# A hybrid convolution/mLSTM block on one core: x normalised in place, the width-31 convolution accumulated in PSUM, modulation sums delayed

## The chip, the cores and the metric

The kernel runs as one program on one core of a Trainium2 chip. A core has a matrix engine (PE, whose weight loads are listed as PEld), a vector engine (DVE), a scalar engine (ACT), a general engine (POOL) and a queue engine that only issues transfers (SP). Each takes its own instructions strictly in order; semaphores tie them together. The metric is the device time of one execution, in microseconds. Of the kernel before three executions were timed: median 1197.08, from 1196.81 to 1198.6. The profiled execution is a run of its own, with a time of its own.

## The reference

One layer of a diffusion block on 1024 latent tokens (1024 channels) with a prefix of 256 context tokens. Cut to what the change touches:

```
hx = modulate(rms_norm(x, norm_g[0]), mx[0], mx[1])      # mx = split(silu(c) @ w_ada + b_ada, 6)
hc = modulate(rms_norm(ctx, norm_g[0]), mc[0], mc[1])    # mc = split(silu(c_ctx) @ w_ada + b_ada, 6)
kc, vc, gtc = project_state_inputs(hc, w_in, b_gates)    # context: k, v and gates alone
a, gl, q, k, v, o, g = split(hx @ w_in + ...)            # latent tokens
u = a * sigmoid(gl)                                      # GLU, 512 channels
u = silu(layer_norm(dwconv31_along_rows_of_64(u) + conv_b))
m = bidirectional mLSTM(q, k, v, g, state from ctx)      # 4 heads, chunks of 64
x = x + mx[2] * rms_norm(concat(u, m * sigmoid(o)) @ w_out)
x = x + mx[5] * rms_norm(conv_ffn(modulate(rms_norm(x), mx[3], mx[4])))
```

Everything is float32. A matmul is run as three passes over split operands: hi x hi, hi x lo and lo x hi, with hi the value rounded to the fast matmul type and lo the rest.

## The kernel before

**Start.** The eight tiles of x (128 tokens x 1024) are loaded in two groups. For each tile ACT sums the squares (`x_sq`, L193), POOL makes the reciprocal root, DVE scales the identity by it into a 128x128 diagonal (`x_rs`, L198), and PE multiplies the tile by that diagonal (`x_tr`, L204), which transposes and normalises at once; being an ordinary float32 matmul it takes two instructions for each of 64 blocks. ACT and DVE copy the result out of PSUM (`x_evac`, L212 and L214). In between come the column sums that give the modulation of x: `mod_sum` (L228), a multiply and sum over a 128x1024 tile of `w_ada`, two for each of eight row blocks; then `mod_apply` makes hi and lo of the normalised x.

**Projection.** `glu0`, then three more GLU blocks, keep PE busy to about 127 us. A second set of 16 `mod_sum`s gives the modulation of the context. `glu_evac` (L274) leaves `u[j]`, 128 channels by 1024 tokens, for each of four channel groups j.

**Convolution.** `conv(j)` starts the accumulator `accf[:, j]` in SBUF with the centre tap and bias on ACT (L278), and adds 30 taps on DVE (L286), each a multiply and add over 16 rows of 64-|o| columns, o from -15 to 15. The four convolutions are given the lowest priority and fill DVE wherever the scheduler finds it idle; `conv_norm` reads them, at about 293 us.

**vpass(1).** PE projects v and gates, ten token tiles: eight of the latent tokens first (t = 2 to 9), then the two context tiles (t = 0, 1), 24 matmuls each (L556 and L557 with hi, L558 with lo). The context operand `hcT` is made late: DVE reads the transposed context out of PSUM and modulates it (L358, tile `h_1287` and three like it), ACT rounds it to hi (L362, tile `s_1280`), DVE subtracts to get lo (L363, tile `s_1281`). Then come vpass(0), the projection of k, the gates, the four heads, the output projection (to about 463 us), and the feed-forward part.

**Sums behind the projection.** 32 further `mod_sum`s (for mx[2] to mx[5]) are spread by `ada_step(2)`, two in each projection step of heads and output gate, and finished before the row at L325 (about 463 us).

**Order.** All engines are ordered by hand up to `glu0(0, 0, (1,))`; from there only SP is, and a list scheduler sets the order of the rest when the program is built, by priorities and its own costs. What each engine is given is fixed then, and none overtakes on the chip. PSUM has eight banks of 128x512: four of pool `mm`, four of pool `tp`.

Of the kernel before, what the change touches and what calls it, by code (L numbers as in the profile page):

```python
# [24 lines left out]
CW = 31  # L25
# [5 lines left out]
def hybrid_block(ctx: ExitStack, tc: tile.TileContext, x, cx, cc, small, gb, w_ada,  # L31
# [10 lines left out]
    wp = wide.enter_context(tc.tile_pool(name="wp", bufs=11, side="right"))  # L42
    rawp = wide.enter_context(tc.tile_pool(name="rawp", bufs=3, side="right"))
    mm = wide.enter_context(tc.tile_pool(name="mm", bufs=4, space=bass.MemoryType.PSUM))
    tp = wide.enter_context(tc.tile_pool(name="tp", bufs=4, space=bass.MemoryType.PSUM))
    early = ExitStack()
    t4 = early.enter_context(tc.tile_pool(name="t4", bufs=10))

# [33 lines left out]
    def MM():  # L82
        return mm.tile([P, 512], F32, tag="mm", name="mm")

    def TP():
        return tp.tile([P, 512], F32, tag="tp", name="tp")

    def H2(n=512):
        return sm.tile([P, 512], F32, tag="h2", name="h2", bufs=8)[:, 0:n]
# [69 lines left out]
    def load_raw(i):  # L159
        r = RAW()  # L160
        sp.dma_start(r, wblk[i])
        return r
# [21 lines left out]
    def x_load(hf):  # L184
        for t in range(4 * hf, 4 * hf + 4):
            xt[t] = T4()
            sp.dma_start(xt[t], x[t * P:(t + 1) * P, :])

    dgx = {}

    def x_sq(t):
        junk = hT[1][1][:, 2 * (t % 4):2 * (t % 4) + 2, :]
        act.activation(out=junk, in_=xt[t].rearrange("p (k n) -> p k n", k=2), func=AF.Square, accum_out=ss[:, t:t + 1])  # L193

    def x_rs(t):
        rsqrt_pow(rst[:, t:t + 1], ss[:, t:t + 1], 1, f"x{t % 2}", 1.0 / D)
        dgx[t] = H2(P)
        dve.tensor_scalar(out=dgx[t], in0=ident, scalar1=rst[:, t:t + 1], scalar2=None, op0=ALU.mult)  # L198

    def x_tr(t, ps, qs=range(4)):  # L200

        for q in qs:
            for kk in range(2):
                pe.matmul(ps[q][:, kk * 256 + t % 2 * P:kk * 256 + (t % 2 + 1) * P],  # L204
                          xt[t][:, (2 * q + kk) * P:(2 * q + kk + 1) * P], dgx[t], start=True, stop=True)

    def x_evac(pr, ps, qs=range(4)):
        for q in qs:
            dst = xT[:, 2 * q:2 * q + 2, pr * 256:(pr + 1) * 256]
            src = ps[q].rearrange("p (k n) -> p k n", k=2)  # L210
            if q % 2:
                dve.tensor_copy(out=dst, in_=src)  # L212
            else:
                act.copy(out=dst, in_=src)  # L214


    def silu_mm(dst):
        pss = MM(), MM()
        for hf in range(2):
            pe.matmul(pss[hf], ones[0:1, :], dst[0:1, hf * 512:(hf + 1) * 512], start=True, stop=True)  # L220
        return pss

    def silu_act(dst, pss):
        for hf in range(2):
            act.activation(out=dst[:, hf * 512:(hf + 1) * 512], in_=pss[hf], func=AF.Silu)
# [49 lines left out]

    def conv(j):
        uv = u[j].rearrange("p (r c) -> p r c", c=W)
        act.activation(out=accf[:, j], in_=u[j], func=AF.Identity, scale=conv_w[:, j, 15:16],  # L278
                       bias=conv_b[:, j:j + 1])
        for t in range(CW):  # L280
            o = t - 15
            if o == 0:
                continue
            lo, hi = max(0, -o), min(W, W - o)
            dst = accf[:, j].rearrange("p (r c) -> p r c", c=W)[:, :, lo:hi]
            dve.scalar_tensor_tensor(out=dst, in0=uv[:, :, lo + o:hi + o], scalar=conv_w[:, j, t:t + 1],  # L286
                                     in1=dst, op0=ALU.mult, op1=ALU.add)


    AB2 = const.tile([P, 2, 8], F32, name="AB2")  # L290
# [106 lines left out]
    with tc.manual_schedule(engines={ET.SP, ET.Activation, ET.DVE, ET.Pool, ET.PE}):  # L397
        sx = SM(1024, "G", bufs=1)
        rows[0] = sx
        sp.dma_start(sx[0:1, :], cc[0:1, :])  # L400
        x_load(0)
        mod_load(0)
        raws = load_raw(0), load_raw(1)
        x_load(1)
        pss = silu_mm(sx)
        x_sq(0)
        x_rs(0)
        pA = [TP() for _ in range(4)]
        x_tr(0, pA)
        x_sq(1)  # L410
        x_rs(1)
        x_tr(1, pA)
        silu_act(sx, pss)
        x_sq(2)
        x_rs(2)
        pB = [MM() for _ in range(4)]
        x_tr(2, pB)
        x_evac(0, pA)
        x_sq(3)
        x_rs(3)  # L420
        x_tr(3, pB)
        mod_k(0)
        x_evac(1, pB)
        x_sq(4)
        x_rs(4)
        pA = [TP() for _ in range(4)]
        x_tr(4, pA)
        mod_apply(0, 0)
        x_sq(5)
        x_rs(5)  # L430
        w = [split_blk(raws[0], dve)]
        w.append(split_blk(raws[1], dve))
        wg[0] = w
        x_tr(5, pA)
        mod_load(1)
        raws = load_raw(2), load_raw(3)
        for k in range(2, KT):
            mod_load(k)
        x_sq(6)
        x_rs(6)  # L440
        mod_sum(ada_raw[1, 1], sx, 0, 1, 1)
        x_evac(2, pA)
        x_sq(7)
        x_rs(7)
        mod_sum(ada_raw[1, 0], sx, 0, 0, 1)
# [4 lines left out]
        for q in range(4):  # L450
            x_tr(6, pA, (q,))
            x_tr(7, pA, (q,))
        mod_s(1)
        mod_apply(1, 0)
        x_evac(3, pA)
        mod_apply(0, 1)
        glu0(0, 1, (0,))
        glu0(0, 0, (1,))
    with tc.manual_schedule(engines={ET.SP}):
        mod_apply(1, 1)  # L460
        glu0(0, 1, (1,))
        wg[1] = split_blk(raws[0], pool), split_blk(raws[1], dve)
# [17 lines left out]
    accf = wide_tile(4, 2)  # L480
    vw = None
    with prio(100000):
        conv(0)
# [195 lines left out]
    def proj(i, evac):  # L679
        w = ahead.pop(i)  # L680
        n = order.index(i) + 1
        if n < len(order):
            ahead[order[n]] = load_blk(order[n])
        ada_step(2)
        for hf in range(2):
            hi, lo = hT[hf]
            ps = MM()
            yield from mm_block(ps, w, hi, lo)
            evac(hf, ps)
        return w  # L690
# [53 lines left out]
    def mlstm_head(h):  # L744
# [38 lines left out]
        for g in range(2):  # L783
# [9 lines left out]
            for t in range(4):  # L793
# [1 line left out]
                    yield from tails()  # L795
                c = 4 * g + t
                cs = slice(c * P, (c + 1) * P)
                pv, pc = TP(), TP()
                nv = pv[:, 0:258].rearrange("p (d n) -> p d n", d=2)
                nc_ = pc[:, 0:258].rearrange("p (d n) -> p d n", d=2)  # L800
                pl.matmul(pc[:, 0:258], qT[:, cs], Cs[c // 4][:, c % 4].rearrange("p d n -> p (d n)"),
# [63 lines left out]
    uf = accf  # L865

    def conv_norm():
        for hf in range(2):
            xh = [T4().rearrange("p (t n) -> p t n", n=512) for _ in range(2)]
            mv = SM(8, "cmv").rearrange("p (t s) -> p t s", s=2)  # L870
# [661 lines left out]
```

## Time and profile before

| | |
|---|---|
| median of the timed runs | 1197.08 us (1196.81 to 1198.6) |
| the profiled execution | 1197.89 us |
| its span, first to last instruction | 1195.8 us |
| PE busy | 1143.2 us, 96% |
| DVE busy | 932.0 us, 78% |
| ACT busy | 523.7 us, 44% |
| POOL busy | 121.3 us, 10% |

The profiled execution's time holds 2.1 us beside its span. A share of busy time is an average over stages with different limits: to see what a change in one stage is worth, one reads that stage's stretch of the span, which engine is full there, and which wait ends last.

### The profile page before, as it was taken

Reading aid. Unit: us, or ns where it says so; the run is one execution under the profiler, and the core shown is the slowest. Engines: PE = TensorE matmul, PEld = TensorE weight load, DVE = VectorE, ACT = ScalarE, POOL = GpSimd, SP = SyncE. Lnnn points to the kernel's source line nnn. Section 1 sums busy time; section 2 is a strip of 40 time slices with the busy share of each in tenths; the row PEclk is TensorE's granted clock in tenths of the full one; section 3 lists DMA queues with packets and bytes.
Section 4 is the critical chain, followed back from the end, with each engine's and each line's share of the span. In section 5 each row is a group of like instructions: output and inputs, shape, how many; then the busy total and the mean of one; then the engine's idle time right before and its main releaser. Section 6 shows DMA issues by size and latency. Waiting matters only on the chain.

```text
span 1195.8 us, 14940 instructions
## 1 busy us (share of the span) xinstructions
PE 1143.2 (96%) x5463; PEld 939.5 (79%) x5463; DVE 932.0 (78%) x1702; ACT 523.7 (44%) x952; POOL 121.3 (10%) x106
## 2 busy tenths in 40 slices
PE   6899898999898999999999999999999999999997
PEld 5788787877687777887787888878888878888885
DVE  4899999999779996568966676676668685995585
ACT  6432222242485454357545344343434355454461
POOL 2634120111302210010000000000000000000000
PEclk9899899999999999999999999999999999999999
DMA  8963110442225412442324231323132159633251
GB/s 305 329 207 121 52 37 1 142 147 65 88 89 176 140 56 89 150 167 89 104 73 132 88 122 55 132 89 132 45 132 93 75 192 391 227 112 117 80 220 71
DMA packets 51823, 153.42 MB, mean 128 GB/s; under 512 B 5589, under 2 KB 5925, under 8 KB 49958
## 3 DMA queue, kind: packets, MB, share of 16 engines
q1 hardware_dynamic: 40662, 132.28, 32.0%
q10 hardware_dynamic: 11088, 20.19, 4.5%
q8 instruction: 43, 0.70, 0.2%
q14 instruction: 30, 0.25, 0.1%
HBM read 123.83 MB, written 28.61 MB: 127 GB/s over the span
## 4 chain that ended last, share of the span: by engine, by line
PE 61%; DVE 6%; ACT 1%; issue 1%; POOL 0%; DVEq 0%; POOLq 0%; ACTq 0%
PE mm L1141 8%; PE mm L1143 8%; PE mm L1142 8%; PE c L1369 3%; PE c L1371 3%; PE c L1370 3%; PE tp L1143 3%; PE tp L1142 3%; PE tp L1141 3%; PE a L1369 3%; PE a L1371 3%; PE a L1370 2%; PE mm L951 2%; PE mm L953 2%; PE mm L952 2%; PE tp L508 2%
## 5 line engine op out<-in xcount | busy, mean ns | idle before, releaser
L286 DVE SCALAR_TENSOR_TENSOR s<-t,sml,s 128x864 f32<-128x864 f32 (+14 forms) x120 | 150.5, 1295 | 0.1
L150 PE MATMUL mm<-s,w 128*128 128x512 f32 (+1 forms) x320 | 126.6, 399 | 0.0
L151 PE MATMUL mm<-s,w 128*128 128x512 f32 (+1 forms) x320 | 124.7, 393 | 0.1
L133 ACT ACTIVATE w<-raw 128x1024 fp32r<-128x1024 f32 x94 | 97.0, 1054 | 20.6 <-DMA raw<-in_w_out_dram 5.3
L1141 PE MATMUL mm<-s,w 128*128 128x512 f32 x264 | 104.9, 397 | 0.7 <-ACT h L1214 0.7
L1142 PE MATMUL mm<-s,w 128*128 128x512 f32 x264 | 104.2, 395 | 0.0
L1143 PE MATMUL mm<-s,w 128*128 128x512 f32 x264 | 104.0, 395 | 0.0
L134 DVE TENSOR_TENSOR w<-raw,w 128x1024 fp32r<-128x1024 f32 x77 | 92.3, 1222 | 1.5 <-PE mm L952 0.8
L154 PE MATMUL mm<-s,w 128*128 128x512 f32 (+1 forms) x320 | 93.2, 400 | 0.0
L141 POOL TENSOR_TENSOR r<-yw,mhalf 128x1 f32<-128x1 f32 x16 | 9.7, 608 | 690.7 <-DVE yw L140 690.7
L1141 PE MATMUL mm<-x,w 128*128 128x512 f32 x176 | 70.5, 401 | 0.7 <-ACT h L1205 0.5
L151 PEld LDWEIGHTS mm<-s,w 128*128 128x128 f32 x320 | 60.9, 190 | 11.6 <-POOL s L265 0.7
L1141 PE MATMUL tp<-s,w 128*128 128x512 f32 x176 | 69.5, 395 | 0.0
L150 PEld LDWEIGHTS mm<-s,w 128*128 128x128 f32 x320 | 61.0, 190 | 10.9
L1142 PE MATMUL tp<-s,w 128*128 128x512 f32 x176 | 69.5, 395 | 0.0
L1143 PE MATMUL tp<-s,w 128*128 128x512 f32 x176 | 69.4, 394 | 0.0
L1142 PE MATMUL mm<-x,w 128*128 128x512 f32 x176 | 69.3, 394 | 0.0
L1143 PE MATMUL mm<-x,w 128*128 128x512 f32 x176 | 69.3, 394 | 0.0
L1197 DVE TENSOR_TENSOR h<-mm,h 128x512 f32<-128x512 f32 x22 | 15.2, 692 | 66.3 <-PE mm L1143 66.3
L1271 ACT ACTIVATE s<-x 128x512 fp32r<-128x512 f32 x62 | 38.4, 628 | 64.1 <-PE a L1371 25.0
L1256 DVE TENSOR_TENSOR s<-x,s 128x512 fp32r<-128x512 f32 x62 | 42.8, 695 | 29.0 <-ACT s L1271 29.0
L154 PEld LDWEIGHTS mm<-s,w 128*128 128x128 f32 x320 | 57.0, 189 | 10.2
(311 smaller groups left out, 2916.6 us busy)
## 6 DMA issues: line engine op xcount, KB each, us to landing
raw<-in_w_up_dram SPq DMA_DIRECT2D x44, 512.0 KB, 4.5
zv<-s ACTq DMA_DIRECT2D x77, 256.0 KB, 3.4
raw<-in_w_ada_dram SPq DMA_DIRECT2D x32, 512.0 KB, 4.2
t<-in_w_ada_dram SPq DMA_DIRECT2D x28, 512.0 KB, 5.8
x<-zv SPq DMA_DIRECT2D x14, 1024.0 KB, 5.0
raw<-in_wblk_dram SPq DMA_DIRECT2D x20, 512.0 KB, 4.8
d<-in_w_down_dram SPq DMA_DIRECT2D x28, 256.0 KB, 6.8
x<-zv SPq DMA_DIRECT2D x7, 768.0 KB, 4.2
```

The costliest lines, as they stand in the source:

```text
L133: act.activation(out=hi, in_=raw, func=AF.Copy)
L134: (eng or pool).tensor_tensor(out=lo, in0=raw, in1=hi.bitcast(F32), op=ALU.subtract)
L150: pe.matmul(o, w[0][:, k], hi[:, k], start=(k == 0), stop=False)
L151: pe.matmul(o, w[0][:, k], lo[:, k], start=False, stop=False)
L154: pe.matmul(o, w[1][:, k], hi[:, k], start=False, stop=(k == KT - 1))
L286: dve.scalar_tensor_tensor(out=dst, in0=uv[:, :, lo + o:hi + o], scalar=conv_w[:, j, t:t + 1], in1=dst, op0=ALU.mult, op1=ALU.add)
L1141: pe.matmul(ps, w[0][:, s], b[0][:, k], start=(start and k == 0), stop=False, skip_group_check=True)
L1142: pe.matmul(ps, w[0][:, s], b[1][:, k], start=False, stop=False, skip_group_check=True)
L1143: pe.matmul(ps, w[1][:, s], b[0][:, k], start=False, stop=(k == 3), skip_group_check=True)
L1369: pe.matmul(ps, o[:, 0, s], o[:, 2], start=start, stop=False, skip_group_check=True)
L1370: pe.matmul(ps, o[:, 0, s], o[:, 3], start=False, stop=False, skip_group_check=True)
L1371: pe.matmul(ps, o[:, 1, s], o[:, 2], start=False, stop=stop, skip_group_check=True)
```

## The change

1. PSUM. `tp` falls from four banks to two; a new pool `cv` holds one pair of banks. While no convolution runs, `TP()` hands out halves of the pair for two requests of every four. While one runs (`conv_live`), the pair is the convolution's, and head 0 takes one of its banks from `mm` (`HP()`).
2. Start of x. DVE scales the whole tile in place (128x1024), PE transposes it with the plain identity as a transpose, one instruction a block; the order of steps and of evacuations is changed; the SiLU is taken on the one row before it is spread to 128 partitions. The loads are reordered: SP issues the modulation weights ahead of the fourth weight block.
3. Convolution. The centre tap is a DVE operation from SBUF to PSUM, 29 taps read and write PSUM, the last tap (o = 1) writes `accf` in SBUF, and a 128x16 copy fills the column that it misses. There is one pair of banks, so the four convolutions follow one another.
4. Sums. `ada_step(2)` in each of twelve steps becomes `ada_step(4)` in the last six or so (`n > 5`) and none before.

```diff
-    tp = wide.enter_context(tc.tile_pool(name="tp", bufs=4, space=bass.MemoryType.PSUM))
+    tp = wide.enter_context(tc.tile_pool(name="tp", bufs=2, space=bass.MemoryType.PSUM))
+    cv = wide.enter_context(tc.tile_pool(name="cv", bufs=1, space=bass.MemoryType.PSUM))
...
+    def CV():
+        return cv.tile([P, 2, 512], F32, tag="cv", name="cv")
...
     def TP():
+        if not conv_live:
+            tp_turn[0] += 1
+            if tp_turn[0] % 4 in (3, 0):
+                if not halves_left:
+                    pair = CV()
+                    halves_left.extend((pair[:, 1], pair[:, 0]))
+                return halves_left.pop()
         return tp.tile([P, 512], F32, tag="tp", name="tp")
+    def HP():
+        return MM() if conv_live else TP()
...
-        dgx[t] = H2(P)
-        dve.tensor_scalar(out=dgx[t], in0=ident, scalar1=rst[:, t:t + 1], scalar2=None, op0=ALU.mult)
+        dve.tensor_scalar(out=xt[t], in0=xt[t], scalar1=rst[:, t:t + 1], scalar2=None, op0=ALU.mult)
...
-                pe.matmul(ps[q][:, kk * 256 + t % 2 * P:kk * 256 + (t % 2 + 1) * P],
-                          xt[t][:, (2 * q + kk) * P:(2 * q + kk + 1) * P], dgx[t], start=True, stop=True)
+                pe.transpose(ps[q][:, kk * 256 + t % 2 * P:kk * 256 + (t % 2 + 1) * P],
+                             xt[t][:, (2 * q + kk) * P:(2 * q + kk + 1) * P], ident)
...
     def silu_mm(dst):
+        act.activation(out=dst[0:1, :], in_=dst[0:1, :], func=AF.Silu)
...
     def conv(j):
         uv = u[j].rearrange("p (r c) -> p r c", c=W)
-        act.activation(out=accf[:, j], in_=u[j], func=AF.Identity, scale=conv_w[:, j, 15:16],
-                       bias=conv_b[:, j:j + 1])
-        for t in range(CW):
+        pair = CV().rearrange("p h n -> p (h n)")
+        pv = pair.rearrange("p (r c) -> p r c", c=W)
+        fv = accf[:, j].rearrange("p (r c) -> p r c", c=W)
+        dve.tensor_scalar(out=pair, in0=u[j], scalar1=conv_w[:, j, 15:16], scalar2=conv_b[:, j:j + 1], op0=ALU.mult,
+                          op1=ALU.add)
+
+        for t in (*range(15), *range(17, CW), 16):
             o = t - 15
-            if o == 0:
-                continue
             lo, hi = max(0, -o), min(W, W - o)
-            dst = accf[:, j].rearrange("p (r c) -> p r c", c=W)[:, :, lo:hi]
+            dst = (fv if o == 1 else pv)[:, :, lo:hi]
             dve.scalar_tensor_tensor(out=dst, in0=uv[:, :, lo + o:hi + o], scalar=conv_w[:, j, t:t + 1],
-                                     in1=dst, op0=ALU.mult, op1=ALU.add)
+                                     in1=pv[:, :, lo:hi], op0=ALU.mult, op1=ALU.add)
+        dve.tensor_copy(out=fv[:, :, W - 1:W], in_=pv[:, :, W - 1:W])
...
-        ada_step(2)
+        ada_step(4 if n > 5 else 0)
...
-                pv, pc = TP(), TP()
+                pv, pc = TP(), HP()
```

Lines after the change stand some 13 to 21 further down (L363 is L384, L286 is L306, L556 is L569).

**DVE, at the context operand of vpass(1), before** (`t_725` and `t_732` are the inputs of convolutions 0 and 1, which alternate):

```order
L565 COPY h_1111<-mm 128x2x2x4
L286 SCALAR_TENSOR_TENSOR s_739<-t_725,sml,s_739 128x16x57
L286 SCALAR_TENSOR_TENSOR s_739<-t_732,sml,s_739 128x16x59
L286 SCALAR_TENSOR_TENSOR s_739<-t_725,sml,s_739 128x16x56
L565 COPY h_1111<-mm 128x2x2x4
L358 TENSOR_SCALAR h_1287<-tp,AB 128x256 x2
L358 TENSOR_SCALAR h_1297<-tp,AB 128x256 x2
L363 TENSOR_TENSOR s_1281<-h_1287,s_1280 128x512
L358 TENSOR_SCALAR h_1307<-tp,AB 128x256
L363 TENSOR_TENSOR s_1281<-h_1297,s_1280 128x512
```

**DVE, the same operand after**, in two places (`t_724` is the input of convolution 1, `t_811` that of convolution 2):

```order
L578 COPY h_1111<-mm 128x2x2x4
L379 TENSOR_SCALAR h_1287<-tp,AB 128x256 x2
L379 TENSOR_SCALAR h_1297<-tp,AB 128x256 x2
L379 TENSOR_SCALAR h_1307<-tp,AB 128x256 x2
L379 TENSOR_SCALAR h_1317<-tp,AB 128x256 x2
L636 MEMSET h_1664 1x256
L306 SCALAR_TENSOR_TENSOR cv<-t_724,sml,cv 128x16x61
```

```order
L306 SCALAR_TENSOR_TENSOR cv<-t_811,sml,cv 128x16x50
L306 SCALAR_TENSOR_TENSOR cv<-t_811,sml,cv 128x16x49
L306 SCALAR_TENSOR_TENSOR s_732<-t_811,sml,cv 128x16x63
L384 TENSOR_TENSOR s_1281<-h_1287,s_1280 128x512
L384 TENSOR_TENSOR s_1281<-h_1297,s_1280 128x512
L384 TENSOR_TENSOR s_1281<-h_1307,s_1280 128x512
L384 TENSOR_TENSOR s_1281<-h_1317,s_1280 128x512
L308 COPY s_732<-cv 128x16
```

The subtractions for `s_1281` stood two places behind the modulation, with 43 taps ahead of them on DVE; they now stand behind all 90 taps of convolutions 0, 1 and 2.

**PE, at the first context tile of vpass(1), after:**

```order
L571 MATMUL mm<-w,s_118 128x272
L569 MATMUL mm<-w,s_1280 128x272 [waits Activation_49]
L570 MATMUL mm<-w,s_1280 128x272
L569 MATMUL mm<-w,s_1280 128x272 [waits DVE_49]
L570 MATMUL mm<-w,s_1280 128x272
L569 MATMUL mm<-w,s_111 128x256 [waits DVE_49]
L571 MATMUL mm<-w,s_1281 128x272 [waits DVE_49]
```

Only one matmul of a later stage (with `s_111`) has been put ahead of the one that reads `s_1281`; everything else stays behind it, as before.

**SP, the loads of the start, before** (`w` and `t_288` on are the modulation weights, `raw` the weight blocks, `t_145` to `t_151` tiles of x):

```order
L187 DMA t_151<-in_x_dram 128x1024
L243 DMA w<-in_w_ada_dram 128x1024 x2
L161 DMA raw<-in_wblk_dram 128x1024 x2
L243 DMA t_288<-in_w_ada_dram 128x1024
L243 DMA t_290<-in_w_ada_dram 128x1024
```

and after:

```order
L207 DMA t_154<-in_x_dram 128x1024
L261 DMA w<-in_w_ada_dram 128x1024 x2
L181 DMA raw<-in_wblk_dram 128x1024
L261 DMA t_162<-in_w_ada_dram 128x1024
L261 DMA t_164<-in_w_ada_dram 128x1024
L181 DMA raw<-in_wblk_dram 128x1024
L261 DMA t_168<-in_w_ada_dram 128x1024
```

The fourth weight block, which reuses the buffer of the first, has moved behind two of the modulation loads.

## Rows read from the trace of the kernel before

**Rows 1.** The page: span, then busy us, share and instructions of each engine.

```profile
span 1195.8 us, 14940 instructions
...
PE 1143.2 (96%) x5463; PEld 939.5 (79%) x5463; DVE 932.0 (78%) x1702; ACT 523.7 (44%) x952; POOL 121.3 (10%) x106
```

**Rows 2.** Busy us (instructions) of PE, PEld, DVE, ACT, POOL by stretch; clock, DMA.

```profile
120.00:164.70 44.70, 38.76 (x253) 35.81 (x251) 44.10 (x52) 11.77 (x26) 4.36 (x3) 0.92 0.12 36
164.70:220.00 55.30, 47.65 (x324) 43.95 (x324) 55.02 (x80) 13.10 (x38) 8.53 (x6) 0.94 0.06 20
220.00:308.50 88.50, 81.03 (x443) 67.64 (x441) 87.66 (x175) 26.57 (x67) 17.93 (x6) 1.00 0.36 120
308.50:463.00 154.50, 147.17 (x816) 121.73 (x817) 131.26 (x488) 89.71 (x214) 26.51 (x20) 1.00 0.36 119
```

**Rows 3.** DVE, then PE, at the context operand: start, us, instruction, idle before, releaser.

```profile
162.35 0.68 DVE L363 TENSOR_TENSOR s<-h,s 128x512 fp32r<-128x512 f32 x1
...
163.09 0.39 PE L558 MATMUL mm<-w,s 128*128 128x272 f32 x1
...
164.21 0.39 PE L556 MATMUL mm<-w,s 128*128 128x272 f32 x1 [0.35 <-ACT s L362]
...
165.05 0.39 PE L558 MATMUL mm<-w,s 128*128 128x272 f32 x1 [0.32 <-DVE s L363]
```

**Rows 4.** Convolution taps alone (L286), by stretch: DVE busy us (instructions), clock, DMA.

```profile
97.60:120.00 22.40, 21.30 (x14) 1.00 0.39 108
120.00:164.70 44.70, 34.28 (x30) 0.92 0.12 36
164.70:220.00 55.30, 45.79 (x40) 0.94 0.06 20
220.00:308.50 88.50, 49.16 (x38) 1.00 0.36 120
```

**Rows 5.** SP's longest wait up to 60 us: what waits, total, times, longest.

```profile
SPq L161 <- DVE w L134: 10.0, 1, 10.0
```

**Rows 6.** DVE by shape, whole span: form, count, busy us, mean ns, idle before.

```profile
L286 DVE SCALAR_TENSOR_TENSOR s<-t,sml,s 128x896 f32<-128x896 f32 x8 | 9.1, 1142 | 0.0
L1037 DVE TENSOR_SCALAR t<-t,r 128x1024 f32<-128x1024 f32 x8 | 6.0, 753 | 5.7 <-POOL r L141 5.7
L358 DVE TENSOR_SCALAR h<-tp,AB 128x256 f32<-128x256 f32 x8 | 3.9, 534 | 0.0
L565 DVE COPY h<-mm 128x16 f32<-128x16 f32 x10 | 1.8, 175 | 0.0
L228 DVE SCALAR_TENSOR_TENSOR raw<-raw,G 128x1024 f32<-128x1024 f32 x32 | 38.7, 1213 | 0.1
```

**Rows 7.** The same view: two operations with a PSUM source, one between SBUF tiles.

```profile
L821 DVE SCALAR_TENSOR_TENSOR h<-tp,dn,h 128x128 f32<-128x128 f32 x96 | 31.9, 345 | 0.1
L1197 DVE TENSOR_TENSOR h<-mm,h 128x512 f32<-128x512 f32 x22 | 15.2, 692 | 66.3 <-PE mm L1143 66.3
L1119 DVE TENSOR_TENSOR w<-h,w 128x512 fp32r<-128x512 f32 x22 | 15.1, 686 | 0.1
```

**Rows 8.** DVE and POOL in time, where the first taps run.

```profile
97.62 8.97 DVE L286 SCALAR_TENSOR_TENSOR s<-t,sml,s 128x784 f32<-128x784 f32 x3
...
97.60 5.51 POOL L134 TENSOR_TENSOR w<-raw,w 128x1024 fp32r<-128x1024 f32 x2 [16.47 <-ACT w L133]
```

**Rows 9.** The page's group of all 120 taps: busy us, mean ns, idle before.

```profile
L286 DVE SCALAR_TENSOR_TENSOR s<-t,sml,s 128x864 f32<-128x864 f32 (+14 forms) x120 | 150.5, 1295 | 0.1
```

**Rows 10.** PE in time, behind a wait early in vpass(1).

```profile
141.47 0.60 PE L556 MATMUL mm<-w,s 128*128 128x272 f32 x1 [3.57 <-DVE t L274]
...
142.09 0.43 PE L558 MATMUL mm<-w,s 128*128 128x272 f32 x1
```

**Rows 11.** PE's waits from 164.7 to 308.5: total us, times, longest.

```profile
PE tp L508 <- DVE h L821: 4.5, 4, 1.5
PE tp L508 <- DVE gsc L617: 3.4, 1, 3.4
```

More of the change, by code (lines that the diff above doesn't have):

```diff
@@ L83, in MM @@
         return mm.tile([P, 512], F32, tag="mm", name="mm")
-    def TP():
+    def CV():
+        return cv.tile([P, 2, 512], F32, tag="cv", name="cv")
+    conv_live = []
+    halves_left = []
+    tp_turn = [0]
+    def TP():
+        if not conv_live:
[5 more added lines that the diff above has]
+                return halves_left.pop()
         return tp.tile([P, 512], F32, tag="tp", name="tp")
+    def HP():
+        return MM() if conv_live else TP()
     def H2(n=512):
@@ L203, in x_tr, with x_evac @@
             for kk in range(2):
-                pe.matmul(ps[q][:, kk * 256 + t % 2 * P:kk * 256 + (t % 2 + 1) * P],
-                          xt[t][:, (2 * q + kk) * P:(2 * q + kk + 1) * P], dgx[t], start=True, stop=True)
-    def x_evac(pr, ps, qs=range(4)):
-        for q in qs:
+                pe.transpose(ps[q][:, kk * 256 + t % 2 * P:kk * 256 + (t % 2 + 1) * P],
+                             xt[t][:, (2 * q + kk) * P:(2 * q + kk + 1) * P], ident)
+    def x_evac(pr, ps, dq=(1, 3)):
+        for q in range(4):
             dst = xT[:, 2 * q:2 * q + 2, pr * 256:(pr + 1) * 256]
             src = ps[q].rearrange("p (k n) -> p k n", k=2)
-            if q % 2:
+            if q in dq:
                 dve.tensor_copy(out=dst, in_=src)
@@ L221, in silu_mm, with silu_rows @@
         return pss
-    def silu_act(dst, pss):
+    def silu_rows(dst, pss):
         for hf in range(2):
-            act.activation(out=dst[:, hf * 512:(hf + 1) * 512], in_=pss[hf], func=AF.Silu)
+            act.copy(out=dst[:, hf * 512:(hf + 1) * 512], in_=pss[hf])
     def mod_sum(r, s, w, ch, k):
@@ L402, in hybrid_block, with x_in @@
         mod_load(0)
-        raws = load_raw(0), load_raw(1)
+        raws = [load_raw(0), load_raw(1)]
         x_load(1)
+        mod_load(1)
+        raws.append(load_raw(2))
+        mod_load(2)
+        raws.append(load_raw(3))
+        for k in range(3, KT):
+            mod_load(k)
         pss = silu_mm(sx)
-        x_sq(0)
-        x_rs(0)
+        def x_in(t, ps):
+            x_sq(t)
+            x_rs(t)
+            x_tr(t, ps)
         pA = [TP() for _ in range(4)]
[L409 to L415, printed above, removed]
-        pB = [MM() for _ in range(4)]
[L417 to L422, printed above, removed]
+        x_in(0, pA)
+        x_in(1, pA)
+        silu_rows(sx, pss)
+        pB = [MM() for _ in range(4)]
+        x_in(2, pB)
+        x_in(3, pB)
+        x_evac(0, pA, ())
+        mod_sum(ada_raw[0, 1], sx, 0, 1, 0)
         x_evac(1, pB)
[L424 to L427, printed above, removed]
+        mod_sum(ada_raw[0, 0], sx, 0, 0, 0)
+        mod_s(0)
+        w = [split_blk(raws[0], dve)]
         mod_apply(0, 0)
-        x_sq(5)
-        x_rs(5)
-        w = [split_blk(raws[0], dve)]
         w.append(split_blk(raws[1], dve))
         wg[0] = w
[L434 to L445, printed above, removed]
         for hf in range(2):
@@ L449, in hybrid_block @@
         pA = [TP() for _ in range(4)]
[L450 to L453, printed above, removed]
+        x_in(4, pA)
+        x_in(5, pA)
+        x_evac(2, pA)
+        pA = [TP() for _ in range(4)]
+        x_in(6, pA)
+        x_in(7, pA)
+        mod_k(1)
+        x_evac(3, pA)
         mod_apply(1, 0)
-        x_evac(3, pA)
         mod_apply(0, 1)
@@ L461, in hybrid_block @@
         glu0(0, 1, (1,))
-        wg[1] = split_blk(raws[0], pool), split_blk(raws[1], dve)
+        wg[1] = split_blk(raws[2], pool), split_blk(raws[3], dve)
         for hf in range(2):
@@ L480, in hybrid_block @@
     accf = wide_tile(4, 2)
+    conv_live.append(True)
     vw = None
@@ L867, in conv_norm @@
     def conv_norm():
+        conv_live.clear()
         for hf in range(2):
```

1 line of the change is left out of this document (removed).

## The prediction

> **What bounds the kernel now.** I read the page's first part first: PE is busy 1143.2 of 1195.8 us, DVE 932.0 [rows 1]. So PE sets the time, and a change is worth what it adds to or takes from PE's idle time. The table of busy time by stretch then tells where PE is not full [rows 2]. Behind 463 us it nearly is; between 164.7 and 308.5 it is idle for 55.30 - 47.65 + 88.50 - 81.03 = 15.1 us, and there DVE is busy 55.02 + 87.66 = 142.7 of 143.8 us. The list of PE's waits there names DVE's results first [rows 11]. So from the start of the convolution to 308 us DVE is the engine that is full, and the place of one DVE instruction in its queue matters. The taps alone take DVE 150.5 us [rows 9], 94.95 of them in that stretch [rows 4].
>
> The third view is PE in time at 163 us, where vpass(1) reaches the context tiles. The first lo subtraction runs on DVE at 162.35, PE reads its result at 163.09, and PE waits 0.35 and 0.32 us for ACT and DVE in this place [rows 3]. Before, this is just in time: it has no slack to speak of.
>
> **Convolution and its place in the order: the term that decides.** The order of DVE shows the four subtractions that PE needs behind 90 taps, where they stood behind 43. PE takes its queue in order and has one matmul of a later stage ahead of the first that waits, so everything from the context tiles on waits for these taps. Nothing covers that. The start of the first subtraction, from 162.35 [rows 3]:
>
> - 47 more taps at 1.142 us, the mean of the middle size, 128x896, which is also the mean size of the 30 taps [rows 6]: +53.7.
> - Three first operations of a convolution, SBUF to PSUM, which ACT did before: no row has this form; the 128x1024 scaling between SBUF tiles takes 0.753 [rows 6]: +2.3 (with a tap's 1.142 instead, +3.4).
> - Four more context modulations at 0.534 and three more copies at 0.175 now stand ahead [rows 6]: +2.7.
> - The first 14 taps took 21.30 us, 1.52 each, the next 30 took 34.28, 1.14 each [rows 4]; while POOL worked, three took 8.97 [rows 8]. Taps with an operand in PSUM ran 345 ns a piece in 96 cases [rows 7], which leaves no room for such a stretch. I take it as gone: -5.3 (0 at the other end).
> - The start stage, below: -5.
>
> The sum is 210.8. The subtraction takes 0.7, so PE goes on at 211.5 where it went on at 163.09: +48.4. The 1.0 us or so that it loses there now is then inside the wait; I take **+47**.
>
> No row has a tap in PSUM, so 1.142 is bounded. Below: a 128x128 operation with one PSUM operand takes 345 ns and a 128x512 one 692 [rows 7], 0.904 ns an element; carried on to 896 elements this is 1.039, over 90 taps 9.3 us less. Above: the mean of all 120 taps with their stretches, 1.295 [rows 9], 13.8 us more. I keep 1.142 because PSUM as a source costs nothing at equal size: 692 against 686 ns [rows 7]. With the start at 0 or -9 us, the first subtraction comes at 197 to 230.
>
> [...]
>
> [...]
>
> **What comes back.** When PE goes on, 90 taps are done instead of 43. DVE has 30 taps, some 34 us, left where it had 94.95 [rows 4], and six sums fewer to run before `conv_norm` (8 instead of 14), 6 x 1.21 = 7.3 us [rows 6]. Its load up to `conv_norm` falls from 142.7 to about 75 us, and it no longer bounds the stretch. PE can recover its idle 15.1 us and the lower clock at 164.7 to 220, 0.94 or 6.6 us at half speed, 3.3 us [rows 2]: 18.4. The chain of the gates keeps a part of its waits (3.4 us on `gsc` alone [rows 11]), against which stand gaps too short to be listed as idle. I take **-18**, from -10 to -22.
>
> **Delayed sums.** Of the 32 sums, 20 instead of 18 now fall between `conv_norm` and the row at L325, four at the end. DVE is busy 131.26 of 154.50 us in that stretch, PE idle 7.3 [rows 2]; two sums are 2.4 us of DVE work [rows 6], part of it on the path: **+1**, from -4 to +5. The same bounds hold what two `tp` banks less cost the heads, since no row shows a bank as what a matmul waits for.
>
> **The start.** The in-place scaling costs DVE eight operations of 0.75 instead of the small ones, PE saves half of its 128 instructions, ACT a table load. SP waited 10.0 us in one piece for a buffer, with the modulation loads behind it [rows 5]; these now go ahead. So the sums that lead up to the convolution can start earlier, by at most those 10 us; DVE is their limit more than the loads, and I take 5, from 0 to 9. This is already in the sum: it does not shorten the time by itself, as PE waits at 154 or so in any case.
>
> **Sum.** 47 + 3.6 - 18 + 1 = +33.6. The profiled execution took 1197.89 us, 2.1 more than its span and 0.8 more than the median of 1197.08. 1197.08 + 33.6 gives 1230.7; I say **1231**. Ends: first subtraction at 197 and full recovery, 33 + 3.6 - 22 - 4 = +11, 1208; at 230 and little recovery, 66 + 3.6 - 10 + 5 = +65, 1262. Both ends at once are unlikely.
>
> **Rivals.**
>
> *A, faster: the taps run fast.* If operations on PSUM ran like the 128x1024 scaling, 0.753 us or 0.66 for 896 elements [rows 6], the 90 taps would end by 163. It decides from here: 210.8 less 90 x (1.142 - t) must fall to 163, t = 0.61 us. [...] Against it: a tap has two tensor sources, and such an operation with one in PSUM takes 692 ns for only 512 elements [rows 7]. Chance 0.07. [...]
>
> *B, no change that can be measured.* The wait comes, but what comes back pays for it. That needs 51 us of slack behind it; 18.4 in the stretch and PE's idle 7.3 us up to 463 [rows 2] make 25.7. So it needs taps near 0.9 us besides. Chance 0.03, at 1197 to 1200.
>
> *C, slower still.* Taps that depend on one another through a single pair of banks cannot alternate, as two convolutions do now. If each pays 0.15 us for that, the wait is 13.8 us longer (the upper end above), and if two `tp` banks also hold up the heads, little comes back: 1197 + 61 + 3.6 - 8 + 2 = 1256. For it: today only pairs alternate, and no row shows a chain alone. Against: 345 ns for 128 elements leaves no extra cost in PSUM [rows 7]. Chance 0.14.
>
> *D, the change does not do what it says:* the order of the queues is fixed, so this could only be a part of the gain at the start that does not come; it is inside the range.
>
> **How the numbers follow.** The forecast has 0.76 (1213 to 1248), A 0.07, B 0.03, C 0.14. The range of 8 in 10 leaves out A, B, most of the forecast's lowest corner and the upper part of C: 1207 to 1257. A difference of 0.2% (2.4 us) is about what a measurement of this kernel can tell from no change. Faster by more than that: A and a corner of a shorter wait, 0.09. Within it: 0.03. Slower: 0.88.
>
> **What would show it.** In the profile after, PE should have one long idle piece that starts between 150 and 160 us and ends when the line of the lo subtraction (L384) releases it, near 211. The mean of the tap group should be near 1.14 us, with no 3 us ones among the first. DVE should show free time between 212 and `conv_norm`, PE nearly none. Behind 500 us nothing should differ. If PE has no idle piece over 10 us there, the central step is wrong; if the piece is there and the time is still under 1205, what comes back was read too small; if taps are above 1.25 us, C holds.

## The result, and the profile after

The changed kernel takes 1291.28 us (1285.18 to 1293.06) against 1197.05, a ratio of 1.0775 with the interval 1.0736 to 1.0814. The direction was as forecast; the loss is 94 us, not 34, and the time lies above the range (1207 to 1257).

All views of the changed kernel are of an execution of 1285.18 us, the fastest of the four. Its page, as in [rows 1] and [rows 9], with PE's group at the wait:

```profile
span 1283.4 us, 14751 instructions
...
PE 1151.7 (90%) x5399; PEld 937.2 (73%) x5399; DVE 949.9 (74%) x1708; ACT 522.1 (41%) x950; POOL 117.5 (9%) x106
...
L306 DVE SCALAR_TENSOR_TENSOR cv<-t,sml,cv 128x784 f32<-128x784 f32 (+14 forms) x116 | 133.3, 1149 | 3.2
...
L571 PE MATMUL mm<-w,s 128*128 128x272 f32 (+1 forms) x160 | 46.9, 294 | 51.8 <-DVE s L384 51.8
```

PE has nearly the same work, and 131.7 us of its span (1283.4 - 1151.7) are idle where 52.6 were before. The table by stretch, as [rows 2], tells where (PE, PEld, DVE, ACT, POOL, then clock, DMA share, GB/s):

```profile
120.00:164.70 44.70, 36.27 (x228) 33.36 (x227) 42.81 (x52) 7.19 (x19) 3.48 (x4) 0.92 0.12 36
164.70:220.00 55.30, 5.91 (x45) 5.47 (x44) 53.03 (x49) 2.95 (x8) 0.00 (x0) 0.57 0.00 0
220.00:308.50 88.50, 85.05 (x546) 76.80 (x547) 56.26 (x97) 30.94 (x84) 14.63 (x9) 0.96 0.13 43
308.50:400.00 91.50, 83.47 (x451) 66.98 (x450) 55.72 (x183) 39.42 (x87) 17.66 (x14) 0.98 0.36 121
400.00:550.00 150.00, 122.67 (x603) 97.59 (x602) 123.19 (x422) 63.22 (x151) 15.74 (x9) 0.93 0.33 106
```

There are two holes, not one. The first is the forecast wait: PE stands from 171.7 to 223.45 us. Here are DVE and then PE in time at its end, as [rows 3]:

```profile
220.45 1.04 DVE L306 SCALAR_TENSOR_TENSOR cv<-t,sml,cv 128x784 f32<-128x784 f32 x1
221.53 1.26 DVE L306 SCALAR_TENSOR_TENSOR s<-t,sml,cv 128x1008 f32<-128x1008 f32 x1
222.71 2.49 DVE L384 TENSOR_TENSOR s<-h,s 128x512 fp32r<-128x512 f32 x4
...
223.45 0.59 PE L571 MATMUL mm<-w,s 128*128 128x272 f32 x1 [51.79 <-DVE s L384]
223.84 0.43 PE L569 MATMUL mm<-w,s 128*128 128x272 f32 x1
```

The last tap of convolution 2 (the one that writes SBUF) is followed by the four subtractions, and PE goes on. The second hole, 27 us of PE between 400 and 550, was not forecast. PE's waits there, in total, times, longest:

```profile
PE cv L521 <- DVE h L834: 15.5, 6, 8.1
PE tp L521 <- DVE h L834: 7.2, 4, 3.0
```

L521 issues the matmuls of the heads, and L834 is the instruction with which DVE reads a chunk's banks of PSUM; its output is the tile `h`. The longest case is the first scores of a group of chunks:

```profile
478.23 2.05 PE L521 MATMUL cv<-t,t 128*128 128x128 f32 x8 [8.12 <-DVE h L834]
```

Their inputs (tiles `t`) are no product of L834. What PE waits for is the *bank*. (Of the 22.7 us in the two rows, 5.6 stand before matmuls that read a tile of `h`; for these the profile alone cannot tell bank from data.)

The start of the same matmul in both traces, in microseconds, shows how the delay grows:

```
                                     before    after   later by
first matmul of vpass(1)              126.9    133.1      6.2
last matmul of vpass                  208.5    259.9     51.4
last matmul of the projections        431.5    506.6     75.1
first matmul of the gate row          462.8    541.2     78.4
first matmul of the feed-forward      537.7    622.7     85.0
last of that loop                     976.1   1063.3     87.2
```

So 51 us are there when vpass ends. Where the projections end they have become 75, at the start of the feed-forward 85: instead of 18 us coming back, 34 more are lost.

### The profile page after: what moved, and what is told of

Same layout as the page of the kernel before. It is cut to its first block, busy times and chain, and to the rows that moved or that the text cites. A ratio compares the mean times of both kernels' runs of the same rounds, so it can differ in the third digit from the quotient of the medians.

```text
span 1283.4 us, 14751 instructions
## 1 busy us (share of the span) xinstructions
PE 1151.7 (90%) x5399; PEld 937.2 (73%) x5399; DVE 949.9 (74%) x1708; ACT 522.1 (41%) x950; POOL 117.5 (9%) x106
## 4 chain that ended last, share of the span: by engine, by line
PE 57%; DVE 10%; DMA 3%; ACT 3%; issue 1%; POOL 1%; DVEq 0%; POOLq 0%; ACTq 0%
PE mm L1155 7%; PE mm L1157 7%; PE mm L1156 7%; DMA raw<-in_w_ada_dram 3%; PE c L1385 3%; PE c L1384 3%; PE c L1383 3%; PE a L1385 2%; PE a L1384 2%; PE a L1383 2%; PE mm L965 2%; PE mm L966 2%; PE mm L967 2%; PE cv L521 1%; PE tp L1155 1%; PE tp L1156 1%
## 5 line engine op out<-in xcount | busy, mean ns | idle before, releaser
L170 PE MATMUL mm<-s,w 128*128 128x512 f32 (+1 forms) x320 | 131.5, 414 | 7.4 <-ACT s L282 4.3
L306 DVE SCALAR_TENSOR_TENSOR cv<-t,sml,cv 128x784 f32<-128x784 f32 (+14 forms) x116 | 133.3, 1149 | 3.2
L171 PE MATMUL mm<-s,w 128*128 128x512 f32 (+1 forms) x320 | 128.0, 403 | 0.9 <-POOL s L283 0.9
L571 PE MATMUL mm<-w,s 128*128 128x272 f32 (+1 forms) x160 | 46.9, 294 | 51.8 <-DVE s L384 51.8
L174 PE MATMUL mm<-s,w 128*128 128x512 f32 (+1 forms) x320 | 89.7, 397 | 0.0
L170 PEld LDWEIGHTS mm<-s,w 128*128 128x128 f32 x320 | 62.7, 196 | 19.4 <-ACT s L282 4.9
L171 PEld LDWEIGHTS mm<-s,w 128*128 128x128 f32 x320 | 62.6, 196 | 13.0 <-POOL s L283 2.3
L571 PEld LDWEIGHTS mm<-w,s 128*128 128x128 f32 x160 | 31.4, 197 | 52.0 <-DVE s L384 52.0
L174 PEld LDWEIGHTS mm<-s,w 128*128 128x128 f32 x320 | 57.5, 190 | 11.1
L154 POOL TENSOR_TENSOR w<-raw,w 128x1024 fp32r<-128x1024 f32 x17 | 44.8, 2643 | 162.1 <-ACT w L153 40.0
```

The source lines that it names most:

```text
L154: (eng or pool).tensor_tensor(out=lo, in0=raw, in1=hi.bitcast(F32), op=ALU.subtract)
L170: pe.matmul(o, w[0][:, k], hi[:, k], start=(k == 0), stop=False)
L171: pe.matmul(o, w[0][:, k], lo[:, k], start=False, stop=False)
L174: pe.matmul(o, w[1][:, k], hi[:, k], start=False, stop=(k == KT - 1))
L571: pe.matmul(o, lo[:, k], w[0], start=False, stop=(k == KT - 1))
```

## The experiments

Labels that begin with a_ are the changed kernel with an edit, those with b_ the kernel before with one. Times are medians; each ratio is to the kernel before on the same chip.

### The long wait: the place of the subtractions

a_touch adds, after `accf` is made:

```diff
     accf = wide_tile(4, 2)
+    for j in (0, 2):
+        pool.memset(accf[:, j, 0:1], 0.0)
```

> The changed kernel, with two 128x1 memsets on POOL that write one column of each accumulator tile (accf) right after the tiles are made. In the built order the four lo subtractions then stand behind 42 taps again, not 90. Theory 1 (the place of the subtractions makes the long wait): PE's wait for L384, 51.8 us in the changed kernel, falls under 2 us, and the time falls by 45 to 55 us, to 1236 to 1246, since the later loss between the heads and the gate row (some 36 us) has another cause. Rival 1 (the convolution in PSUM is simply too much for DVE, and its 120 taps are waited for wherever they stand): another wait of the same size appears before 310 us, and the time stays above 1265.

It took 1240.46 us, 1.0367 (1.0345 to 1.0389): 51 us less than the changed kernel. PE has no wait for L384 left; its largest waits are now those of the second hole:

```profile
PE cv L523 <- DVE h L836: 15.5, 7, 8.4
PE tp L523 <- DVE h L836: 7.5, 5, 2.3
```

Theory 1 holds. The edit also tells why the subtractions went back. In the kernel before ACT wrote the accumulator at the start of each convolution; in the changed one the first write of the second accumulator tile is the last tap of convolution 2, and the subtractions' tiles, which come from the same pool and later in the program, stand right behind that tap. Moving the first write forward moves them forward. That the scheduler gives out a pool's tiles in the order of the program is my reading of this; the order and the time are what was measured.

b_conv puts the convolution in PSUM alone, with the pools that it needs, into the kernel before.

> The kernel before with the convolution in PSUM alone (pools tp and cv, CV(), HP(), the new conv()); start, loads and sums as before. The subtractions stand behind 90 taps here too. Theory 1: the long wait comes, some 45 us of it, and nothing else: 1235 to 1250. Rival (the wait needs the later start of the changed kernel to hurt, as it hides in other waits): under 1215.

1288.77 us, 1.0746 (1.072 to 1.0773). The wait for the subtraction is there (59.0 us), but the time is 40 us above the expectation: this part alone carries the whole loss, and the second hole with it.

### The second hole: not the sums

a_sums2 is the changed kernel with the old spread of sums, a_touch_sums2 is a_touch with it; b_sums4 is the kernel before with the new one, so the same edit the other way round:

```diff
-        ada_step(4 if n > 5 else 0)
+        ada_step(2)
```

> The changed kernel with the modulation sums spread as before, two in each of the twelve projection steps. Theory 2 (four sums in each of the last steps crowd DVE and its loads while the heads run): the 36 us by which the changed kernel falls further behind between the third head and the gate row go, so the time falls to about 1255 (1248 to 1265), and DVE's 15.8 us of waits for w_ada loads there go under 5. Rival 2 (fewer banks in pool tp, or the order of the heads that the late start brings): the loss stays, 1280 or more.

> Both edits: the accumulator touched early, and two sums in each step. Theories 1 and 2 together: only the 6 us lost up to the projection (133.1 against 126.9 us) stay, against which stands DVE's free time up to the convolution's norm: 1195 to 1206. If PSUM taps, which follow one another at 1.187 us where two alternating SBUF chains follow at 1.14, or the two missing tp banks matter: 1215 or more.

> The kernel before with the modulation sums delayed alone (four in each of the last six steps). The pairs so far say from 6 us faster to 5 us slower: 1191 to 1203. If the crowding of DVE by the late sums were what costs the heads 36 us: 1220 or more.

Measured: 1285.94 (1.073, 1.0711 to 1.0748), 1246.72 (1.0408, 1.0392 to 1.0423) and 1205.83 (1.0068, 1.0053 to 1.0084). Theory 2 falls: with the old spread the changed kernel loses nearly as much (5 us less, with intervals that overlap), and a_touch loses 6 us more. In the trace of the changed kernel DVE did wait 15.8 us for those sums' loads in this stretch, and it did run sums between the reads that PE needed; but in a_sums2 these waits are 21.8 us instead of under 5, and the loss stays. b_sums4 lies 3 us above its range.

### The second hole: the pools

b_pool is the kernel before with the pools of the changed one (two `tp` banks, one pair) and the convolution in SBUF.

> The kernel before with the new PSUM pools alone: two tp banks and one pair whose halves are handed out in turn, a new pair only when both halves of the last are free; the convolution stays in SBUF, so it never holds the pair. Theory 3 (the joint release of the pair, and the fixed turn of four, stall the heads between the third head and the gate row, which is where every kernel with these pools fell behind by 25 to 50 us): 1222 to 1245, with PE waits for the heads' readers (lines of h, dn and t) of more than 20 us in all between 360 and 500 us. Rival 3 (the heads run late or in another order because the convolution ends late): 1195 to 1205.

1248.37 us, 1.0422 (1.0403 to 1.0442): the pools alone cost 51 us, 3 more than the top of the range. From 400 to 460 us, in the columns of the table above:

```profile
400.00:420.00 20.00, 14.84 (x71) 12.28 (x72) 15.22 (x43) 11.95 (x29) 3.40 (x2) 0.74 0.64 215
420.00:440.00 20.00, 13.18 (x68) 9.61 (x66) 17.90 (x65) 5.10 (x8) 1.01 (x1) 0.93 0.46 143
440.00:460.00 20.00, 13.44 (x53) 10.46 (x54) 17.72 (x64) 13.41 (x33) 0.00 (x0) 0.76 0.30 99
```

No engine is full there, and PE's granted clock is 0.74, 0.93 and 0.76 (1.00, 1.00 and 0.91 in b_two, below): the heads wait in turn for each other's engines. a_touch_halves and b_conv_touch_halves keep one pair after the convolutions and reuse its halves one by one (the list is also emptied where the convolutions begin):

```diff
                 if not halves_left:
                     pair = CV()
-                    halves_left.extend((pair[:, 1], pair[:, 0]))
-                return halves_left.pop()
+                    halves_left.extend((pair[:, 0], pair[:, 1]))
+                return halves_left[tp_turn[0] % 4 == 0]
```

> The kernel a_touch with one pair that is kept after the convolutions and whose two halves are reused each by itself, so that a matmul into one half waits for readers of that half alone. Theory 3: of the 50 us that a_touch loses from the third head to the gate row most goes, 1190 to 1210. Rival 3: 1230 or more.

> The kernel before with the convolution in PSUM, the accumulator touched early and the halves independent; start, loads and sums as before. Theory 3 and no loss at the start: 1183 to 1200, since PE's early waits for glu_evac go and DVE has less left behind the context tiles. Rival 3: 1230 or more.

1242.76 (1.0375, 1.0356 to 1.0395) and 1246.35 (1.0406, 1.039 to 1.0422): no gain. Next, b_pool_mm, a_touch_mm and b_conv_touch_mm take the bank `pc` of each chunk from pool `mm`:

```diff
     def HP():
-        return MM() if conv_live else TP()
+        return MM()
```

> The kernel b_pool (before, with two tp banks and the pair, the convolution in SBUF), but every chunk of a head takes its bank pc from pool mm (HP() always gives MM()). Theory 4 (of four banks in two kinds that are handed out in a fixed turn each chunk holds two, so a chunk waits for the readers of an earlier one, and the 51 us of b_pool are such waits): 1195 to 1212. Rival 4 (the banks are enough, and the heads are slow because the list scheduler puts DVE's and ACT's work for them in a worse order): 1235 or more.

> The kernel a_touch with pc from pool mm for every head. Theory 4: the 50 us that it loses from the third head to the gate row shrink to under 15, 1190 to 1208. Rival 4: 1230 or more.

> The kernel before with the convolution in PSUM, the accumulator touched early, pc from pool mm; start, loads and sums as before. Theory 4: the 8 to 12 us by which the kernels with a touched accumulator lead up to 320 us are kept: 1182 to 1197, faster than before. Rival 4: 1230 or more.

1242.53 (1.0379, 1.0363 to 1.0394), 1239.31 (1.0348, 1.0331 to 1.0366) and 1249.56 (1.0436, 1.0421 to 1.0452). Theory 4 falls too. What separates them is b_two: the same two kinds in the same fixed turn, but as single-bank tiles.

```diff
-    cv = wide.enter_context(tc.tile_pool(name="cv", bufs=1, space=bass.MemoryType.PSUM))
+    cv = wide.enter_context(tc.tile_pool(name="cv", bufs=2, space=bass.MemoryType.PSUM))
...
-        return cv.tile([P, 2, 512], F32, tag="cv", name="cv")
+        return cv.tile([P, 512], F32, tag="cv", name="cv")
...
-                if not halves_left:
-                    pair = CV()
-                    halves_left.extend((pair[:, 1], pair[:, 0]))
-                return halves_left.pop()
+                return CV()
```

> The kernel before with the four tp banks split into two pools of two single banks, handed out in the fixed turn of b_pool (two from the one, two from the other); no pair, convolution in SBUF, nothing else changed. If it is the fixed turn between two kinds of banks that costs the heads 45 to 51 us (theory 5): 1235 to 1255. If it is the pair, two banks that come free only together (theory 3): 1195 to 1210.

1203.26 us, 1.0039 (1.0027 to 1.005), 45 us below b_pool. The same stretch:

```profile
400.00:420.00 20.00, 19.75 (x105) 16.00 (x105) 18.79 (x75) 8.00 (x23) 1.92 (x1) 1.00 0.55 172
420.00:440.00 20.00, 17.31 (x100) 14.31 (x98) 19.07 (x69) 11.21 (x30) 1.31 (x1) 1.00 0.09 27
440.00:460.00 20.00, 18.04 (x82) 14.69 (x83) 18.82 (x75) 9.71 (x17) 1.92 (x1) 0.91 0.26 81
```

So neither the number of banks nor the turn costs much; the two-bank *tile* does. The built programs say how. Each matmul into a half of the pair carries waits; in b_pool 48 of them name a reader of the *other half of the same pair*, and 37 a reader of the other half of the pair before. In a_touch_halves, with one pair throughout, 67 name the other half. In b_two there is no other half to wait for. The dependencies are kept per tile: two banks in one tile work as one bank, so `tp` had three. This explains why a_touch_halves gained nothing: the halves shared a tile there too. How much of the 51 us PE loses in these waits, and how much through the order that the scheduler makes of the whole program under the same dependencies (rival 4), the runs do not separate: from some 310 us to the gate row PE's waits for the chunk reads come to 11.6 us in b_pool against 3.1 in the kernel before, all its listed waits to 34.2 against 8.3.

a_touch_pools, b_conv_touch_pools and a_touch_pools_sums2 use this: the two banks are a two-bank tile only while convolutions run.

```diff
+    def cv_open(bufs):
+        cvs[0].close()
+        cvs[1:] = [cvs[0].enter_context(tc.tile_pool(name="cv", bufs=bufs, space=bass.MemoryType.PSUM))]
+
+    cv_open(2)
...
+                return cvs[1].tile([P, 512], F32, tag="tq", name="tq")
...
     conv_live.append(True)
+    cv_open(1)
...
         conv_live.clear()
+        cv_open(2)
```

> The kernel a_touch, but the two banks are opened as two single-bank tiles of a pool before and after the convolutions, and as one two-bank tile only while the convolutions run. Theory 6 (in the built programs most matmuls into one half of a pair wait for a reader of the other half, in b_pool as in a_touch_halves: a pair works as one bank, tp as three): the loss of a_touch behind 340 us goes, 1188 to 1203. If the taps in PSUM or the serial convolutions cost the heads something besides: 1215 or more.

> The same on the kernel before: convolution in PSUM, accumulator touched early, single-bank tiles outside the convolutions; start, loads and sums as before. Theory 6 with no loss at the start and none from delayed sums: 1183 to 1197, faster than before by up to 14 us. Otherwise 1215 or more.

> The kernel a_touch_pools with two sums in each projection step, as before. On the kernel before the delayed sums cost 8 us, in a_touch they gained 6. If they cost only where the heads do not wait for banks: 5 to 9 us less than a_touch_pools. If they help wherever the convolution runs in PSUM, since DVE is fuller early: 3 to 8 us more.

1209.41 (1.0103, 1.0086 to 1.0121), 1217.52 (1.0166, 1.0146 to 1.0185) and 1216.7 (1.0162, 1.0145 to 1.0179). a_touch falls by another 31 us, to a time between the two ranges given. In a_touch_pools PE waits 5.0 and 4.6 us for the chunk reads where a_touch waited 7.5 and 15.5:

```profile
PE tp L527 <- DVE h L840: 5.0, 4, 2.0
PE tq L527 <- DVE h L840: 4.6, 4, 2.1
```

Some 12 us remain, and b_conv_touch_pools missed its first range by 20 us and lies in the second. The delayed sums gain 7 us in this pair, as the second reading had it. b_conv_touch_mmsplit and a_touch_mmsplit leave `tp` its four banks and split `mm` instead (two banks and the pair, in the same turn):

> The kernel before with the convolution in PSUM and the accumulator touched early, but the pair is taken out of pool mm (two banks and the pair in turn) and tp keeps its four. Theory 5 or 3 (the split of tp is what costs the heads): the loss behind 340 us goes or is small, as mm's tiles are few and long, and the early gain of 8 to 12 us stays in part: 1185 to 1205. If any split of PSUM reorders the heads for the worse: 1225 or more.

> The same in the changed kernel (new start, delayed sums): 0 to 10 us more than b_conv_touch_mmsplit, 1188 to 1210, if the start's 5.6 us and the delayed sums' 8 us, as measured on the kernel before, partly add up. If any split of PSUM costs the heads: 1225 or more.

1229.89 (1.026, 1.0245 to 1.0276) and 1231.95 (1.0283, 1.0265 to 1.03): both in the second range, so a pair in `mm` costs too, though less than one in `tp` (b_conv_touch_halves took 1246.35). The place fits: `mm` carries much of the feed-forward, and between the first and the last matmul of that loop these two fall from 11.3 and 7.4 us behind the kernel before to 30.3 and 28.7, where no other run loses more than 4.

### The start

b_x is the kernel before with the new start alone.

> The kernel before with the new start alone (x scaled in place, transposes, the row's SiLU, the order of the loads). All kernels with this start stood 5 to 8 us behind at 126 us, half of it given back by 140. If that loss lasts: 1199 to 1206. If the early waits of vpass(1) absorb it: 1195 to 1199. The prediction's 5 us earlier start of the convolution would give under 1195.

1203.43 us, 1.0048 (1.0033 to 1.0063): the new start loses 5.6 us, of which 3.5 are there at the last matmul of vpass. In the changed kernel PE waits 6.18 us in one piece in the start, and from 20 to 40 us its granted clock is 0.67 (0.83 in the kernel before):

```profile
32.67 1.09 PE L221 MATMUL tp<-ident,t 128*128 128x128 f32 x4 [6.18 <-DVE x1w L160]
```

L160 is DVE's small step of the row norm of an x tile. The profile names the step `x1w`, that of the next tile; what the transposes read is the tile that L215 scales, and its own step, `x0w`, stands in DVE's order behind modulation sums, one of which waits for its load and takes 3.29 us:

```profile
25.41 3.29 DVE L246 SCALAR_TENSOR_TENSOR t<-t,G 128x1024 f32<-128x1024 f32 x1 [0.89 <-DMA t<-in_w_ada_dram]
...
30.97 0.14 DVE L160 TENSOR_SCALAR x0w<-ssx 128x1 f32<-128x1 f32 x1
...
31.77 0.75 DVE L215 TENSOR_SCALAR t<-t,rstx 128x1024 f32<-128x1024 f32 x1 [0.39 <-POOL rstx L161]
```

b_x has this wait too, of 6.05 us, but so has the kernel before, of 4.69:

```profile
32.90 5.87 PE L204 MATMUL tp<-h,t 128*128 128x128 f32 x28 [4.69 <-DVE h L198]
```

So it is not the whole of the loss. In b_x PE also waits 4.30 us, up to 18.99, for ACT's rounding of the modulated x (L262); the longest such wait in the kernel before is 2.83. No run takes these apart. And a_touch_pools_sums2 and b_conv_touch_pools, which differ in the start alone, take 1216.7 and 1217.52 us: there it costs nothing.

## Why the prediction was wrong

**The deciding term was right in kind and nearly in size.** 90 taps, a wait that ends with L384, the first subtraction at 222.71, within the bounds of 197 to 230, and PE goes on at 223.45 where 211.5 was forecast. Taking the wait away was worth 51 us; 47 and 3.6 in the sum make 50.6 (in part by luck, since the wait itself was longer and some of it came back). One row was misread: the subtraction at 162.35 is the second. The first stands a microsecond earlier, and PE waits for it:

```profile
161.30 0.68 DVE L363 TENSOR_TENSOR s<-h,s 128x512 fp32r<-128x512 f32 x1
...
162.03 0.39 PE L558 MATMUL mm<-w,s 128*128 128x272 f32 x1 [0.25 <-DVE s L363]
```

From there the same terms give 210.4 for PE, 13.0 us less than measured. In DVE's trace they are: the convolution starts at 100.07 us and not at 92.6, +7.5; the first operations of three convolutions take 4.15 us in all, up to the next instruction, and not 2.3, +1.9; the 90 taps take 106.1 us where 43 took 55.5, so 50.6 more where 53.7 less 5.3 was forecast, +2.2; small instructions make the rest, 1.4.

**POOL's stretch did not go; it moved.** The taps were not stretched, as forecast: the first eight took 9.03 us, and three of them ran beside POOL. But POOL's work now begins 10 us earlier, on top of the last sums ahead of the convolution, and three of these take 3.42, 3.41 and 2.92 us where 1.21 is usual. These 6.1 us are most of the 7.5:

```profile
87.33 6.29 POOL L154 TENSOR_TENSOR w<-raw,w 128x1024 fp32r<-128x1024 f32 x2 [4.13 <-ACT w L153]
93.58 2.90 POOL L403 TENSOR_TENSOR w<-raw,w 128x816 fp32r<-128x816 f32 x1
...
91.29 3.41 DVE L246 SCALAR_TENSOR_TENSOR t<-t,t 128x1024 f32<-128x1024 f32 x1
...
100.07 1.35 DVE L299 TENSOR_SCALAR cv<-t,sml 128x1024 f32<-128x1024 f32 x1
101.45 9.03 DVE L306 SCALAR_TENSOR_TENSOR cv<-t,sml,cv 128x784 f32<-128x784 f32 x8
```

The new start is not what delays the convolution: in b_x the first tap runs at 96.05 us, 1.6 earlier than in the kernel before, and in b_conv, with the old start, two such sums are stretched and the convolution starts at 101.83.

**A tap costs its queue something else than its mean duration.** Taps of two convolutions in turn began 1.06 us after one another (unstretched, mean), each some 80 ns before the record of the one ahead ends; taps of one chain begin 1.187 us apart. So the chain costs 0.12 us a tap, and 1.142 lay between the two. Three taps in turn, each of 1.16 us, in the kernel before:

```profile
156.15 3.33 DVE L286 SCALAR_TENSOR_TENSOR s<-t,sml,s 128x912 f32<-128x912 f32 x3
```

A tap's own mean time rose by only 12 ns at the size 128x896 (1154 against 1142).

**The clock.** No run shows the 3.6 us that the sum adds to the 47; they were my estimate. In their place the changed kernel shows a granted clock of 0.50 from 223.45 to 227.24 us, right behind the long wait: there some 17 matmuls start 0.227 us apart instead of 0.126, about 1.7 us.

**The step that failed: "What comes back" and, in "Delayed sums", the bounds for the banks.** I wrote that DVE would no longer bound the stretch, which is so (56.26 of 88.50 us up to 308.5), and took 18 us back from it. PE went on 61.4 us late (223.45 against 162.03) and was 51.4 late at the end of vpass, so 10 us did come back; from there the delay only grew, by 34 us up to the feed-forward. Some gain is real once the wait is gone: at the end of vpass a_touch is 3.2 us ahead of the kernel before, b_conv_touch_pools 10.2. But the term took nothing off for the banks. I gave the two missing banks -4 to +5 us "since no row shows a bank as what a matmul waits for". [Rows 11] showed just that: `PE tp L508 <- DVE h L821`. The matmul writes `tp`, and L821 reads `tp`; none of these four matmuls reads `h`, which L821 writes, as here:

```profile
282.76 0.71 PE L508 MATMUL tp<-w,t 128*128 128x129 f32 x4 [1.51 <-DVE h L821]
```

A matmul that waits for an instruction that *reads* its output tile, and makes none of its inputs, is waiting for a bank. With four separate banks that was 4.5 us up to 308.5 and 1.9 behind it. I read the line as a wait for DVE's result, and so put nothing for the banks into the sum and no more than 5 us into its upper end.

The size of this term could not have come from the rows alone, since the change of two banks into one tile has no row before. But the upper bound should have come from the stretch in which those banks are used: if three banks carry what four did, a third of the 154.5 us up to 463 [rows 2] could be lost, 51 us, and not 5. b_pool measured 51 us, a_touch to a_touch_pools 31. That the bound meets the 51 is luck: PE, not the banks, filled that stretch before (147.17 us of it).

**Delayed sums: +1 was forecast.** Measured, +8 in the kernel before, +5 in the changed one, -6 and -7 in a_touch and a_touch_pools: a small term, whose sign differs from kernel to kernel. Why, no run shows.

**The start: -5 was forecast for the sums, 0 for the time.** It costs 5.6 us by itself. The loads went ahead as forecast, and with them the sums went ahead of the last x tiles on DVE, for which PE waits; the forecast left that queue out. What part of the 5.6 us is lost there stays open.

**The rivals.** A and B did not happen. A's own 0.66 us a tap missed its condition of 0.61: the first subtraction would still have come at 167. C named both mechanisms, the dependent taps (0.12 us each against two in turn, 0.045 against the 1.142 of the sum, where it took 0.15) and the two `tp` banks, at 1256 and with a chance of 0.14. Its price for the banks was 10 us of lost recovery; the banks alone cost three to five times that.

**What is open.** Without the wait and the pair, 12 us remain in a_touch_pools, 20 in b_conv_touch_pools. The second is 10.2 us ahead of the kernel before at the last matmul of vpass and 11.9 behind at the last of the projections. On the way PE waits 7.1 us for the norm of the convolution, where the kernel before waits 1.5, in pieces such as

```profile
320.26 0.48 PE L538 MATMUL tp<-ident,t 128*128 128x128 f32 x1 [2.82 <-ACT t L916]
```

and the last tap runs at 314.7 us, in the kernel before at 307.1. So the serial convolutions may end too late for it; this was not tried by itself, and most of the 22 us lies elsewhere. No version was found that beats the kernel before.

## What to carry to other kernels

When an edit changes buffers, read every wait for an instruction that reads the waiting instruction's output tile, and makes none of its inputs, as a wait for a buffer, and price the edit from those lines and from the stretch they stand in. Two banks allocated as one tile were here one buffer to everything that waited (b_pool took 1248.37 us, b_two 1203.26); join them only while they are used as one. And when the first write of a tile moves, look in the built order at what else takes tiles from the same pool: here a store that moved to the end of a loop took four unrelated subtractions with it, and two one-column memsets brought 51 us back.

## What the runs showed that I had not expected

An operation between SBUF and PSUM on DVE cost hardly more than one within SBUF when it has two tensor sources (1154 against 1142 ns at 128x896), but the single-source scaling did: 1.35 us at 128x1024 into PSUM (with two scalars), 0.753 within SBUF (with one). And taps with an accumulator in PSUM were not stretched while POOL worked: the first eight took 1.13 us each, and none of the twelve that ran beside POOL's longer operations took over 1.2 us. With the accumulator in SBUF ten taps took 2.2 to 3.3 us, all of them beside POOL; the first three took 8.97 us together [rows 8].
